# Differential attention: the scores of both maps matmul by matmul in turn on the two halves of TensorE's rows

## The chip, the cores and the metric

One NeuronCore of a Trainium2 chip runs the program. The metric is the device time of one execution in microseconds; the time shown for a kernel is the median of its runs.

## The reference

A decoder trunk of two layers over 528 tokens (16 learned ones ahead of 512) with 1024 channels, all float32. Each layer is half a SwiGLU feed-forward, a mixing sub-layer, and another half feed-forward. The mixing sub-layer projects the normalised input once and gives the parts to two groups of four heads: retention (rq, rk, rv, rg) and differential attention (dq, dk, dv). The change touches the differential group, cut here to what matters:

```
for nb in range(n_blocks):                       # query blocks of 128 (the first has 16 tokens)
    n_keys = (nb + 1) * CHUNK
    qb = q[:, :, :, nb * CHUNK:(nb + 1) * CHUNK] # two maps of 64 channels per head
    s = jnp.einsum('bhmid,bhmjd->bhmij', qb, k[:, :, :, :n_keys]) * scale
    allowed = (kj[None, :] <= qi[:, None]) & (kj[None, :] >= pad)
    p = jax.nn.softmax(jnp.where(allowed, s, -1e30), axis=-1)
    a = p[:, :, 0] - lam * p[:, :, 1]
    outs.append(jnp.einsum('bhij,bhje->bhie', a, v[:, :, :n_keys]))
```

Each head has two score maps; each contracts 64 channels. A softmax is taken of each, and the second, times lambda, is subtracted from the first. The result multiplies the values, and each head's output is normalised.

## The kernel before

Every float32 operand of a matmul is split into a high and a low part, and a product is three matmuls: high x high, low x high, high x low. Activations lie with channels on partitions and tokens along the free dimension, so q and k of one head are tiles of 128 partitions: map 0 on partitions 0 to 63, map 1 on 64 to 127. A score matmul takes 64 of them as its contraction rows.

A layer's mixing stage is `mix_heads`. `proj(name, hd)` computes one projection of one head: 8 channel blocks x 3 products x 2 spans of 264 tokens, 48 matmuls at line 274 (in layer 1 the query-side ones have one span of 512). `evac_rope` takes dq and dk out of PSUM on ScalarE and VectorE, rotates them with four small DMAs and a GpSimd step, and splits them. `evac_v` writes dv to one buffer `vT`, and `v_tokens` (line 691) transposes it.

`diff_scores(hd, mp)` computes one map of one head. Five query blocks (four in layer 1, where the first 16 tokens aren't needed) have 16, 144, 272, 400 and 528 keys. The 528-key block goes to the pair of PSUM banks A in two spans of 264, the others to the pair B: six and twelve matmuls (nine in layer 1), all at line 699. VectorE adds the mask and takes the row maximum while it copies the scores out (line 733), map 0 to the tile `p0`, map 1 to `a_pad`, one buffer each. ScalarE takes the exponentials with the row sums (called at line 741; the profile shows the helper's line 260). `diff_scale` scales map 0 by the reciprocal of its sums on ScalarE (line 759) and then, for map 1, forms map 0 minus lambda times map 1 on VectorE into `a_pad` (line 761). `diff_turn` transposes `a_pad` in two halves (line 785) and splits the result (lines 788 and 792). `pv` multiplies by the values (line 818), and ScalarE copies the output out (lines 826 and 827). `head_norm` sums its squares over channels by matmuls (line 392) and scales.

PSUM has two tags of two buffers, each buffer a pair of banks: `pm` for projections and `pa` for all that is named here.

The loop over heads issues, for head hd with nxt = hd + 1: dq and dk of nxt, v_tokens(hd), the two halves of diff_turn(hd), the front (scores and scaling) of map 0 of nxt, pv(hd), the front of map 1 of nxt, head_norm(hd), dv of nxt. The order in the source is a priority: a scheduler simulates the engines when the program is built, and moves an instruction ahead of one that it holds not to be ready, so that projections fill gaps. On the chip each engine then runs its list in that fixed order.

Of the kernel before, what the change touches and what calls it, by code (L numbers as in the profile page):

```python
# [8 lines left out]
F32 = mybir.dt.float32  # L9
F32R = mybir.dt.float32r  # L10
AF = mybir.ActivationFunctionType
ALU = mybir.AluOpType
# [3 lines left out]
T = 528  # L16
# [41 lines left out]
DIFF_N = [16 + 128 * i for i in range(5)]  # L58
DIFF_OFF = [sum(DIFF_N[:i]) for i in range(5)]
PAD_OFF = [64 * i * (i + 1) for i in range(5)]  # L60
# [137 lines left out]
def trunk(ctx, tc, hT, gains, wgu, wd, win, wout, gnw, sublnw, lam, ret_cs, diff_cs, dtab, mask, out):  # L198
    nc = tc.nc
# [48 lines left out]
    nosync = mybir.DependencyInfo(mybir.DependencyClass.NoSync, mybir.DependencyReason.DATA)  # L248
# [10 lines left out]
    def act_fn(**kw):  # L259
        i = nc.scalar.activation(**kw)  # L260
        tc.add_manual_dep(i.ins, tables["load"].ins.name, nosync, reason="table order")
        tables["users"].append(i)
# [4 lines left out]
    def pair(tag="pa"):  # L267
        return psum.tile([128, 1024], F32, tag=tag, name=tag)
# [19 lines left out]
    def project(mode, srcs, tag="pm"):  # L288

        ps = pair(tag)  # L290
        for k in range(0, len(srcs), 8):
            accumulate(ps, mode, srcs[k:k + 8], W.take(), k, len(srcs))
        return view(ps, mode)
# [22 lines left out]
    blocks, t4 = {}, {}  # L316
# [90 lines left out]
    def norm_end(mode):  # L407
        rsqrt_into(cols(r, mode), col_sum(sums.pop(0), mode), D, mode)
# [205 lines left out]
    def mix_heads(l, mode_next, yh, yl):  # L614
        with tc.tile_pool(name=f"mix{l}", bufs=1, reuse_waits="tile") as pool:
# [6 lines left out]
            a_pad = pool.tile([128, 1920], F32, name="a_pad")  # L622
            msk = acc
# [10 lines left out]
            def scale_cs(kind):  # L634
                for t in cs[kind]:
                    nc.vector.tensor_tensor(out=t, in0=t, in1=r, op=ALU.mult)
# [5 lines left out]
            qk, vv, probs, gate, yn = {}, {}, {}, {}, {}  # L642
# [54 lines left out]
            def scores(out_, pairs, lc, rc, after=None):  # L697
                for n, (a, b) in enumerate(pairs):
                    mm = nc.tensor.matmul(
                        out=out_, lhsT=a[:, lc:lc + 128], rhs=b[:, rc[0]:rc[1]],  # L700
                        start=n == 0, stop=n == len(pairs) - 1,
                    )
                    if n == 0 and after is not None:
                        tc.add_manual_dep(mm.ins, after.ins.name, nosync, reason="one group at a time in a bank")
                return mm

            blocks_i = (4, 3, 2, 1) if q0 else (4, 3, 0, 2, 1)
            i0 = 1 if q0 else 0

            def diff_scores(hd, mp):  # L710
                lp = slice(64 * mp, 64 * mp + 64)
                (qh, ql), (kh, kl) = ([t[lp] for t in qk[n, hd]] for n in ("dq", "dk"))
                A, B = pair(), pair()
                last = {}
                where = {4: A[:, 248:776], 3: B[:, 0:400], 0: B[:, 400:416], 2: B[:, 512:784], 1: B[:, 784:928]}
                for ib in blocks_i:
                    lc = 16 + 128 * (ib - 1) if ib else 0
                    o = where[ib]
                    parts = ((0, 264), (264, 528)) if ib == 4 else ((0, DIFF_N[ib]),)
                    for c0, c1 in parts:  # L720
                        last[ib] = scores(
                            o[:, c0:c1], ((qh, kh), (ql, kh), (qh, kl)), lc, (c0, c1), last.get({0: 3, 1: 2}.get(ib))
                        )
                if mp == 0:
                    s = pool.tile([128, 1360], F32, tag="p0", name="p0")
                    reg = [s[:, DIFF_OFF[i]:DIFF_OFF[i] + DIFF_N[i]] for i in range(5)]
                else:
                    reg = [a_pad[:, PAD_OFF[i] + 112:PAD_OFF[i] + 112 + DIFF_N[i]] for i in range(5)]
                mx = pool.tile([128, 5], F32, tag="mx", name="mx", bufs=3)
                ls = pool.tile([128, 5], F32, tag="ls", name="ls", bufs=4)  # L730
                for ib in blocks_i:
                    n = DIFF_N[ib]
                    nc.vector.tensor_tensor_reduce(
                        out=reg[ib], in0=where[ib],
                        in1=msk[:, T - n:T] if ib else msk[:, 400:416], scale=1.0, scalar=-3e38,
                        op0=ALU.add, op1=ALU.max, accum_out=mx[:, ib:ib + 1],
                    )
                mx, ls = mx[:, i0:], ls[:, i0:]
                nc.vector.tensor_scalar(out=mx, in0=mx, scalar1=-0.125, scalar2=None, op0=ALU.mult)
                for ib in blocks_i:  # L740
                    act_fn(
                        out=reg[ib], in_=reg[ib], func=AF.Exp, scale=0.125, bias=mx[:, ib - i0:ib - i0 + 1],
                        accum_out=ls[:, ib - i0:ib - i0 + 1],
                    )
                probs[hd, mp] = (reg, ls)

            def diff_scale(hd, mp):
                reg, ls = probs[hd, mp]
                nc.vector.reciprocal(out=ls, in_=ls)
                if mp == 1:  # L750
                    nc.vector.tensor_scalar(
                        out=ls, in0=ls, scalar1=nlam[:, l:l + 1], scalar2=None, op0=ALU.mult
                    )
                    reg0 = probs.pop((hd, 0))[0]
                    probs.pop((hd, 1))
                for ib in sorted(blocks_i):
                    lc = ls[:, ib - i0:ib - i0 + 1]
                    if mp == 0:
                        nc.scalar.activation(out=reg[ib], in_=reg[ib], func=AF.Copy, scale=lc)
                    else:  # L760
                        nc.vector.scalar_tensor_tensor(
                            out=reg[ib], in0=reg[ib], scalar=lc, in1=reg0[ib],
                            op0=ALU.mult, op1=ALU.add,
                        )
# [118 lines left out]
            def evac_gate(hd, ps):  # L883
                gate[hd] = cols(a_pad[:, hd * T:(hd + 1) * T] if hd < 3 else swap, qm)
                nc.vector.tensor_tensor(out=gate[hd], in0=ps, in1=cols(r, qm), op=ALU.mult)
# [11 lines left out]
            def load_decay(hd):  # L897
                dtabs[hd] = row(const, "acc1" + "hl"[hd % 2])
                nc.sync.dma_start(out=dtabs[hd], in_=dtab[hd])
# [3 lines left out]
            def proj(name, hd):  # L903
                ps = project(qm if name in ("dq", "rq", "rg") else FULL, xs, "pa" if len(first) == 2 else "pm")
                first.append(name)
                if len(first) == 1:
                    norm_end(FULL)
                    scale_cs("d")
                if name in ("dq", "dk", "rq", "rk"):
                    evac_rope(name, hd, ps)  # L910
                elif name == "rg":
                    evac_gate(hd, ps)
                else:
                    evac_v(name, hd, ps)

            def diff_front(hd, mp):
                diff_scores(hd, mp)
                diff_scale(hd, mp)

            for name in ("dq", "dk", "dv"):  # L920
                proj(name, 0)
            load_cs("r", ret_cs)
            scale_cs("r")
            load_decay(0)
            diff_front(0, 0)
            diff_front(0, 1)
            for hd in range(HEADS):
                nxt = hd + 1
                if nxt < HEADS:
                    proj("dq", nxt)  # L930
                    proj("dk", nxt)
                else:
                    proj("rq", 0)
                    proj("rk", 0)
                v_tokens("dv", hd)
                diff_turn(hd, 0)
                diff_turn(hd, 1)
                if nxt < HEADS:
                    diff_front(nxt, 0)
                    pv("dv", hd)  # L940
                    diff_front(nxt, 1)
                    head_norm("dv", hd)
                    proj("dv", nxt)
                else:
                    vT["rv"] = pool.tile([128, 640], F32, tag="vT", name="vTr")
                    nc.gpsimd.memset(vT["rv"][:, T:640], 0.0)
                    proj("rv", 0)
                    ret_scores(0)
                    pv("dv", hd)
                    v_tokens("rv", 0)  # L950
                    ret_split(0)
                    head_norm("dv", hd)
            for hd in range(HEADS):
                nxt = hd + 1
# [55 lines left out]
    for i, k in enumerate(PAIRED):  # L1010
# [9 lines left out]
        out=ident, in_=ident, pattern=[[-1, 128]], compare_op=ALU.is_equal, fill=0.0, base=0,  # L1020
# [11 lines left out]
    for l in range(DEPTH):  # L1032
        last = l == DEPTH - 1
# [104 lines left out]
```

## Time and profile before

| | |
|---|---|
| median of 3 runs | 2092.46 us (2090.86 to 2094.35) |
| profiled execution, its time | 2090.78 us |
| its span, first to last instruction | 2089.1 us |
| TensorE matmuls, busy | 2012.6 us (96%) |
| VectorE, busy | 1557.1 us (75%) |
| ScalarE, busy | 964.7 us (46%) |
| GpSimd, busy | 393.5 us (19%) |
| mean granted clock of TensorE | 0.991 of 2.4 GHz |

Busy time is the union of an engine's instructions; weight loads overlap matmuls and are counted apart. Matmuls are pipelined, so the time that one takes from the stream is read from start to start and not from its duration.

### The profile page before, as it was taken

The numbers are of one execution on the slowest core, as the hardware profiler recorded it, in microseconds if no ns is written. First come the engines' busy times: TensorE is split into PE (matmuls) and PEld (weight loads), VectorE is DVE, ScalarE is ACT, GpSimd is POOL, SyncE is SP. The second block draws the span as 40 slices with busy tenths as digits, with TensorE's granted clock in tenths as the row PEclk, the third lists the DMA queues.
The fourth block names the chain that finished last, engine by engine and source line by source line (L and its number), as shares of the span: only waits on it lengthen the run. The fifth ranks groups of instructions, "written<-read, shape, count | busy, mean of one in ns | idle before, by whom it ended". The sixth has DMA issues, their size and how long they took to land. (4 is left out here: it accounts for less than half of the span.)

```text
span 2089.1 us, 36950 instructions
## 1 busy us (share of the span) xinstructions
PE 2012.6 (96%) x15262; PEld 1938.1 (93%) x15262; DVE 1557.1 (75%) x2278; ACT 964.7 (46%) x1502; POOL 393.5 (19%) x274
## 2 busy tenths in 40 slices
PE   7999999999999999999989999999999999999996
PEld 7999999999999999999989999998888878898995
DVE  8758766777777876967698686766777788696765
ACT  7424434455436543534555253344553455353443
POOL 0101000444343200100110010014433241010102
PEclk9999999999999999999999999999999999999998
DMA  5232323311212232232223133133211123333231
GB/s 178 97 102 78 115 82 92 125 58 63 71 53 91 92 122 73 92 121 73 89 97 124 64 105 126 61 94 112 68 59 62 61 82 100 101 101 122 80 104 49
DMA packets 57513, 190.10 MB, mean 91 GB/s; under 512 B 7040, under 2 KB 9088, under 8 KB 57344
## 3 DMA queue, kind: packets, MB, share of 16 engines
q1 hardware_dynamic: 56320, 186.66, 27.2%
q8 instruction: 120, 1.97, 0.4%
q10 hardware_dynamic: 1024, 1.08, 0.3%
q14 instruction: 49, 0.40, 0.1%
HBM read 184.53 MB, written 2.10 MB: 89 GB/s over the span
## 5 line engine op out<-in xcount | busy, mean ns | idle before, releaser
L124 POOL TENSOR_TENSOR ws<-ws,wraw 128x512 f32<-128x512 f32 x78 | 122.1, 1566 | 1114.1 <-DVE ws L123 816.7
L99 ACT ACTIVATE whi<-wraw 128x1024 fp32r<-128x1024 f32 (+1 forms) x183 | 187.4, 1032 | 270.1 <-PE pm L274 148.2
L491 PE MATMUL pm<-XH,xhi 128*128 128x264 f32 (+1 forms) x828 | 238.6, 288 | 12.3 <-DVE gu L542 6.9
L491 PE MATMUL pm<-XH,xlo 128*128 128x264 f32 (+1 forms) x828 | 235.8, 285 | 0.0
L491 PE MATMUL pm<-XL,xhi 128*128 128x264 f32 (+1 forms) x828 | 235.8, 285 | 0.0
L491 PE MATMUL pm<-XH,whi 128*128 128x264 f32 (+1 forms) x732 | 210.3, 287 | 7.2 <-DVE gu L469 6.2
L100 DVE TENSOR_TENSOR wlo<-wraw,whi 128x1024 fp32r<-128x1024 f32 (+1 forms) x151 | 188.2, 1248 | 29.3 <-ACT whi L99 28.5
L491 PE MATMUL pm<-XH,wlo 128*128 128x264 f32 (+1 forms) x732 | 207.8, 284 | 0.0
L491 PE MATMUL pm<-XL,whi 128*128 128x264 f32 (+1 forms) x732 | 207.5, 283 | 0.0
L274 PE MATMUL pm<-XH,whi 128*128 128x264 f32 (+1 forms) x768 | 182.2, 305 | 8.8 <-DVE ra L668 7.8
L274 PE MATMUL pm<-XH,wlo 128*128 128x264 f32 (+1 forms) x768 | 179.8, 303 | 0.0
L274 PE MATMUL pm<-XL,whi 128*128 128x264 f32 (+1 forms) x768 | 179.8, 303 | 0.0
L491 PEld LDWEIGHTS pm<-XH,xhi 128*128 128x128 f32 x828 | 156.7, 189 | 17.5 <-DVE gu L469 6.1
L491 PEld LDWEIGHTS pm<-XH,xlo 128*128 128x128 f32 x828 | 157.1, 190 | 0.3
L491 PEld LDWEIGHTS pm<-XL,xhi 128*128 128x128 f32 x828 | 157.1, 190 | 0.0
L491 PEld LDWEIGHTS pm<-XH,whi 128*128 128x128 f32 x732 | 138.1, 189 | 10.1 <-DVE gu L469 8.3
L274 PEld LDWEIGHTS pm<-XH,whi 128*128 128x128 f32 x768 | 125.0, 191 | 16.4 <-ACT whi L99 3.7
L99 ACT ACTIVATE xhi<-ws 128x1024 fp32r<-128x1024 f32 x82 | 86.8, 1059 | 112.2 <-PE pm L491 38.8
L491 PEld LDWEIGHTS pm<-XH,wlo 128*128 128x128 f32 x732 | 138.4, 189 | 0.2
L491 PEld LDWEIGHTS pm<-XL,whi 128*128 128x128 f32 x732 | 138.3, 189 | 0.0
L274 PEld LDWEIGHTS pm<-XL,whi 128*128 128x128 f32 x768 | 124.7, 191 | 4.7
L274 PEld LDWEIGHTS pm<-XH,wlo 128*128 128x128 f32 x768 | 124.6, 191 | 4.5
(266 smaller groups left out, 6060.7 us busy)
## 6 DMA issues: line engine op xcount, KB each, us to landing
wraw<-in_wgu SPq DMA_DIRECT2D x176, 512.0 KB
wraw<-in_wd SPq DMA_DIRECT2D x66, 512.0 KB
wraw<-in_win SPq DMA_DIRECT2D x56, 512.0 KB
wraw<-in_wd SPq DMA_DIRECT2D x32, 384.0 KB
wraw<-in_wout SPq DMA_DIRECT2D x16, 512.0 KB
slabs<-in_hT SPq DMA_DIRECT2D x8, 264.0 KB
out_y<-slabs SPq DMA_DIRECT2D x8, 256.0 KB
acc1h<-in_dtab SPq DMA_DIRECT2D x4, 264.0 KB
```

The costliest lines, as they stand in the source:

```text
L99: self.nc.scalar.activation(out=hi, in_=t, func=AF.Copy)
L100: (eng or self.nc.vector).tensor_tensor(out=lo, in0=t, in1=hi.bitcast(F32), op=ALU.subtract)
L124: nc.gpsimd.tensor_tensor(out=s4, in0=s2, in1=a12, op=ALU.add)
L274: nc.tensor.matmul(out=ps[:, o:o + c1 - c0], lhsT=a, rhs=b[:, c0:c1], start=start and n == 0, stop=stop and n == 2,)
L491: nc.tensor.matmul(out=out_, lhsT=p[:, s], rhs=q, start=k == 0 and n == 0 and what in ("P1", "P2", "P7"), stop=k == 3 and n == 2, skip_gro ...
```

## The change

One call of `diff_scores(hd, part)` now serves both maps. Part 0 computes the 528-key block of both, part 1 the other blocks of both; each part takes two pairs of banks, one for each map. Within a part the matmuls go map 0, map 1, map 0, map 1, and each depends in the schedule on the one before it, without a semaphore, so that the scheduler keeps them in that order. The copies out with mask and maximum follow each part. The exponentials and `diff_scale` of both maps follow part 1. Around it, dv of the next head moves ahead of part 1, and for head 0 dq of head 1 moves between the two parts.

```
-            def diff_scores(hd, mp):
-                lp = slice(64 * mp, 64 * mp + 64)
-                A, B = pair(), pair()
...
+            def diff_scores(hd, part):
...
+                P = [pair(), pair()]
+                if part == 0:
+                    where = [{4: t[:, 248:776]} for t in P]
+                else:
+                    where = [{3: t[:, 0:400], 0: t[:, 400:416], 2: t[:, 512:784], 1: t[:, 784:928]} for t in P]
...
+                for ib in blocks:
...
+                    for c0, c1 in spans:
+                        for n, (x, y) in enumerate(((0, 0), (1, 0), (0, 1))):
+                            for mp in range(2):
+                                q, k = ops[mp]
+                                mm = nc.tensor.matmul(
+                                    out=where[mp][ib][:, c0:c1], lhsT=q[x][:, lc:lc + 128], rhs=k[y][:, c0:c1],
+                                    start=n == 0, stop=n == 2,
+                                )
...
+                                if "turn" in last:
+                                    tc.add_manual_dep(mm.ins, last["turn"].ins.name, nosync, reason="maps in turn")
+                                last[mp, ib] = last["turn"] = mm
+                for mp in range(2):
...
+                    for ib in blocks:
+                        n = DIFF_N[ib]
+                        nc.vector.tensor_tensor_reduce(
...
+                if part == 0:
+                    return
+                for mp in range(2):
...
+                    for ib in blocks_i:
+                        act_fn(
+                            out=reg[ib], in_=reg[ib], func=AF.Exp, scale=0.125, bias=mx[:, ib - i0:ib - i0 + 1],
...
+                    diff_scale(hd, mp)
...
-            diff_front(0, 0)
-            diff_front(0, 1)
+            diff_scores(0, 0)
+            proj("dq", 1)
+            diff_scores(0, 1)
             for hd in range(HEADS):
                 nxt = hd + 1
                 if nxt < HEADS:
-                    proj("dq", nxt)
+                    if hd:
+                        proj("dq", nxt)
                     proj("dk", nxt)
...
                 if nxt < HEADS:
-                    diff_front(nxt, 0)
+                    diff_scores(nxt, 0)
                     pv("dv", hd)
-                    diff_front(nxt, 1)
+                    proj("dv", nxt)
+                    diff_scores(nxt, 1)
                     head_norm("dv", hd)
-                    proj("dv", nxt)
```

## Rows read from the trace of the kernel before

**Rows 1.** The page's first part: each engine's busy time in us, share, instructions.

```profile
PE 2012.6 (96%) x15262; PEld 1938.1 (93%) x15262; DVE 1557.1 (75%) x2278; ACT 964.7 (46%) x1502; POOL 393.5 (19%) x274
```

**Rows 2.** Busy times in the differential heads' stretches of layers 0 and 1.

```profile
395.00:545.00 150.00, 145.96 (x1146) 140.92 (x1145) 112.61 (x219) 77.66 (x174) 62.19 (x43) 1.00 0.22 71
1428.00:1582.00 154.00, 144.81 (x973) 131.21 (x972) 119.03 (x209) 74.11 (x155) 62.42 (x45) 0.99 0.22 69
```

**Rows 3.** TensorE's waits in these stretches: us in total, times, longest.

```profile
PE pm L274 <- DVE ra L668: 3.1, 2, 1.7
...
PE pm L274 <- DVE ra L668: 4.7, 3, 1.8
PE pa L785 <- DVE a_pad L761: 1.7, 2, 1.3
```

**Rows 4.** TensorE's matmuls around one map's scores: start, us, line, shapes, count.

```profile
444.24 0.41 PE L274 MATMUL pm<-XL,whi 128*128 128x264 f32 x2
444.58 0.39 PE L699 MATMUL pa<-kh,qh 64*128 64x264 f32 x1
444.81 0.28 PE L699 MATMUL pa<-kh,ql 64*128 64x264 f32 x1
...
445.29 0.28 PE L699 MATMUL pa<-kl,qh 64*128 64x264 f32 x1
445.50 0.51 PE L274 MATMUL pm<-XH,whi 128*128 128x264 f32 x2
445.84 0.29 PE L274 MATMUL pm<-XH,wlo 128*128 128x264 f32 x1
446.06 0.45 PE L699 MATMUL pa<-kh,qh 64*128 64x400 f32 x1
446.35 0.34 PE L699 MATMUL pa<-kh,ql 64*128 64x400 f32 x1
446.53 0.34 PE L699 MATMUL pa<-kl,qh 64*128 64x400 f32 x1
...
447.17 0.29 PE L699 MATMUL pa<-kh,ql 64*128 64x272 f32 x1
447.30 0.28 PE L699 MATMUL pa<-kl,qh 64*128 64x272 f32 x1
...
447.80 0.39 PE L274 MATMUL pm<-XH,wlo 128*128 128x264 f32 x1
```

**Rows 5.** Weight loads of the 16-column block and the next, same map.

```profile
446.71 0.18 PEld L699 LDWEIGHTS pa<-kh,ql 64*128 64x128 f32 x1
446.82 0.19 PEld L699 LDWEIGHTS pa<-kl,qh 64*128 64x128 f32 x1
446.93 0.19 PEld L699 LDWEIGHTS pa<-kh,qh 64*128 64x128 f32 x1
```

**Rows 6.** ScalarE in one head: exponentials, pv's output copied, map 0 scaled.

```profile
452.18 0.74 ACT L260 ACTIVATE p<-p,mx 128x528 f32<-128x528 f32 x1 [6.42 <-DVE mx L739]
...
454.73 0.59 ACT L826 ACTIVATE osb<-pa 128x528 f32<-128x528 f32 x1
...
456.24 2.16 ACT L759 ACTIVATE p<-p,ls 128x16 f32<-128x16 f32 x5
```

**Rows 7.** TensorE in this head: map 1's last score, the next turn's first transpose.

```profile
458.52 0.27 PE L699 MATMUL pa<-kl,qh 64*128 64x144 f32 x1
...
467.11 0.27 PE L785 MATMUL pa<-ident,a_pad 128*128 128x128 f32 x1
```

**Rows 8.** VectorE in this head: map 1's second part copied out, first and last.

```profile
458.83 0.57 DVE L733 CUSTOM_DVE_ANT_0 a_pad<-pa,acc 128x400 f32<-128x400 f32 x1 [3.78 <-PE pa L699]
...
460.01 0.08 DVE L733 DVE_READ_ACCUMULATOR2_ANT mx<- 128x1 f32 x1
```

More of the change, by code (lines that the diff above doesn't have):

```diff
@@ L708, in mix_heads @@
             i0 = 1 if q0 else 0
-            def diff_scores(hd, mp):
-                lp = slice(64 * mp, 64 * mp + 64)
-                (qh, ql), (kh, kl) = ([t[lp] for t in qk[n, hd]] for n in ("dq", "dk"))
-                A, B = pair(), pair()
+            def diff_scores(hd, part):
+                ops = [
+                    [[t[64 * mp:64 * mp + 64] for t in qk[n, hd]] for n in ("dq", "dk")] for mp in range(2)
+                ]
+                P = [pair(), pair()]
[3 more added lines that the diff above has]
+                    where = [{3: t[:, 0:400], 0: t[:, 400:416], 2: t[:, 512:784], 1: t[:, 784:928]} for t in P]
+                blocks = [ib for ib in blocks_i if ib in where[0]]
@@ L714, in diff_scores @@
                 last = {}
-                where = {4: A[:, 248:776], 3: B[:, 0:400], 0: B[:, 400:416], 2: B[:, 512:784], 1: B[:, 784:928]}
-                for ib in blocks_i:
+                for ib in blocks:
                     lc = 16 + 128 * (ib - 1) if ib else 0
[L718 to L722, printed above, removed]
-                        )
@@ L724, in diff_scores @@
[L724 to L745, printed above, removed]
+                    spans = ((0, 264), (264, 528)) if ib == 4 else ((0, DIFF_N[ib]),)
@@ new lines, in diff_scores @@
+                    for c0, c1 in spans:
[6 more added lines that the diff above has]
+                                )
+                                after = last.get((mp, {0: 3, 1: 2}.get(ib)))
+                                if n == 0 and after is not None:
+                                    tc.add_manual_dep(
+                                        mm.ins, after.ins.name, nosync, reason="one group at a time in a bank"
+                                    )
+                                if "turn" in last:
+                                    tc.add_manual_dep(mm.ins, last["turn"].ins.name, nosync, reason="maps in turn")
+                                last[mp, ib] = last["turn"] = mm
@@ new lines, in diff_scores @@
+                for mp in range(2):
+                    if part == 0:
+                        if mp == 0:
+                            s = pool.tile([128, 1360], F32, tag="p0", name="p0")
+                            reg = [s[:, DIFF_OFF[i]:DIFF_OFF[i] + DIFF_N[i]] for i in range(5)]
+                        else:
+                            reg = [a_pad[:, PAD_OFF[i] + 112:PAD_OFF[i] + 112 + DIFF_N[i]] for i in range(5)]
+                        mx = pool.tile([128, 5], F32, tag="mx", name="mx", bufs=3)
+                        ls = pool.tile([128, 5], F32, tag="ls", name="ls", bufs=4)
+                        probs[hd, mp] = (reg, ls, mx)
+                    reg, ls, mx = probs[hd, mp]
+                    for ib in blocks:
+                        n = DIFF_N[ib]
+                        nc.vector.tensor_tensor_reduce(
+                            out=reg[ib], in0=where[mp][ib],
+                            in1=msk[:, T - n:T] if ib else msk[:, 400:416], scale=1.0, scalar=-3e38,
+                            op0=ALU.add, op1=ALU.max, accum_out=mx[:, ib:ib + 1],
+                        )
@@ new lines, in diff_scores @@
+                if part == 0:
+                    return
+                for mp in range(2):
+                    reg, ls, mx = probs[hd, mp]
+                    mx, ls = mx[:, i0:], ls[:, i0:]
+                    nc.vector.tensor_scalar(out=mx, in0=mx, scalar1=-0.125, scalar2=None, op0=ALU.mult)
+                    for ib in blocks_i:
+                        act_fn(
+                            out=reg[ib], in_=reg[ib], func=AF.Exp, scale=0.125, bias=mx[:, ib - i0:ib - i0 + 1],
+                            accum_out=ls[:, ib - i0:ib - i0 + 1],
+                        )
+                    probs[hd, mp] = (reg, ls)
+                    diff_scale(hd, mp)
@@ L914, in proj @@
                     evac_v(name, hd, ps)
-            def diff_front(hd, mp):
-                diff_scores(hd, mp)
-                diff_scale(hd, mp)
             for name in ("dq", "dk", "dv"):
```

## The prediction

> **What bounds the kernel now.** I read the page's first part, then two stretches of the trace that hold the differential heads of the two layers, then the order on TensorE inside one head. TensorE's matmuls cover 96% of the span and the next engine, VectorE, 75% [rows 1]. In the two stretches TensorE is busy 145.96 of 150 us and 144.81 of 154 us, and VectorE 112.61 and 119.03 [rows 2]. So TensorE sets the end there too, and time taken from it shortens the kernel as long as nothing else comes late. The list of waits says how near that is: in the first layer's heads the longest total is 3.1 us, for the evacuation of a projection, in the second 4.7 us for the same and 1.7 us for transposes that wait for the softmax's last step [rows 3]. The waits are small but there, and those of the second layer say that the chain from one head's scores to its transposes is already nearly as long as the work that hides it.
>
> **What the scores cost.** One map's scores run as two islands among projection matmuls [rows 4]. Projection matmuls start 0.12 us apart (two to a row, rows 0.24 apart). In the first island six matmuls of 264 columns start 0.12 us apart (444.81 to 445.29 is four steps). In the second the 400-column ones start 0.18 apart, the 272-column ones 0.13. The short ones, 16 and 144 columns, are paced by the weight loads, which follow each other 0.11 us apart although a 16-column stream is far shorter [rows 5].
>
> Around an island there is more. From the last two projection matmuls to the first score 0.34 us pass where two take 0.24; from the first score to the second 0.23 where 0.12 would do; from the last score to the next projection 0.21; and the first two projections after it take 0.34 [rows 4]. That is 0.10 + 0.11 + 0.09 + 0.10 = 0.40 us for going from 128 rows to 64 and back, once an island.
>
> The first island lasts 444.58 to 445.50 and the second 446.06 to 447.80 [rows 4]: 0.92 and 1.74 us, each with 0.20 of that 0.40 inside. Streaming is thus 0.72 + 1.54 = 2.26 us a map. The second layer has no 16-column block, three steps of 0.11 fewer: 1.93. Eight maps each: 18.1 + 15.4 = 33.5 us, and 32 islands x 0.40 = 12.8 us. The scores hold 46 us, 2.2% of the span; nothing the change does to them directly can be worth more than about half.
>
> **The change, part by part.** *Fewer islands.* Both maps' 528-key block becomes one run of twelve matmuls, the rest one of 24 (18 in layer 1). Their order is chained, and once the banks are free every operand is there, so I count them as whole: two islands a head in place of four, 16 fewer, 16 x 0.40 = 6.4 us saved. If projections are put between them this is gone.
>
> *Map by map in turn.* No row shows two neighbours on different halves of the rows, so I bound it. At best two neighbours take the time of one: half of 33.5, 16.7 us. At worst each of the alternations, 11 + 23 a head in layer 0 and 11 + 17 in layer 1, 248 in all, drains the array as entering or leaving an island does (0.20): 50 us lost. Between them lies what [rows 5] point to: loads for 64 rows still come 0.11 us apart, one behind the other. If that stays so across the halves, a pair can't be faster than 2 x 0.11 = 0.22 us, however well the streams overlap. Then 264 columns gain 0.02 a pair (0.24 to 0.22), six pairs: 0.12; 400 columns 0.36 to 0.22, three pairs: 0.42; 272 columns 0.26 to 0.22, three pairs: 0.12; 16 and 144 columns nothing. That is about 0.6 us a head, 5 us over eight. I take this: of the three it is the one nearest to a row, since the load spacing is seen, and neither two loads at once nor a drain inside 64-row work is.
>
> The Trainium skill, page "TensorEngine Tiling (Array Packing)", section Tiling Modes, says that a change of tiling mode drains TensorE, a change of tile within a mode does not, and that different tiles can load weights and multiply in parallel. The trace agrees on the first (0.40 us an island) and has nothing on the others. By that rule the alternation would save the 16.7 us of the best case, not 5.
>
> *What moves.* The same vector and scalar instructions run, in another order. Before, map 0's exponentials ran before pv's output was copied: from 452.18 to 454.73, 2.55 us, with the copy of pv's output right behind them [rows 6]. Now no exponential runs before the second part's scores, so that copy, and the bank it frees, come up to 2.55 us sooner. But all of map 0's later work now lands behind the last score. Today the last score starts at 458.52 and the first transpose of the next turn at 467.11, 8.6 us later [rows 7]. Added to that: map 0's reductions of the short blocks, 1.26 us as map 1's from 458.83 to the last read's end at 460.09 [rows 8]; its exponentials, 2.55; its five scaling copies, 2.16 [rows 6]. That is 6.0 us, 14.6 in all. Over it lie dq and dk of the head after next, 48 matmuls x 0.12 = 5.8 us each, and five transposes of v and four matmuls of column sums, 1 us at the same step: 12.7. The next head's dv, another 5.8, can be pulled ahead by the planner as the island gaps show that it pulls projections ahead: 18.5. So it is covered, with little to spare. For head 0, whose dq(1) now stands between its two parts, only dk(1) and dv(1) cover it: 11.6 + 1 against 14.6. Two heads x about 1 to 2 us: I take 2 us lost in all. The planner's rearrangement of weight splits and rotary steps on VectorE and ScalarE I cost at nothing, since they have about 25% and 50% idle time in these stretches [rows 2]; if they fall into the chain they add to it.
>
> dv(nxt) moves ahead of the second part, where it covers the copy of pv's output. Its own evacuation needs v's buffer, free since the transposes of v of this head. No DMA is added; the weights' order is that of the projections, which differs in nothing but dq(1) and dv, so SP's queue stays as it is. Banks: two pairs per part, as two pairs per map before.
>
> Sum: 6.4 + 5 - 2 = 9.4 us saved. The profiled execution took 2090.8 us, so 2081.4; the median of the runs is 1.7 us above that execution, so 2083.
>
> **Rivals.** *Full overlap*, chance 0.22. Two halves load and stream together: 6.4 + 16.7 = 23.1 us off TensorE, 2.9 a head. Then the 18.5 us of cover shrinks against a chain that doesn't, and I take 2 + 4 us lost to it (0.5 a head): 17 us, 2075. For it: the streams touch different rows and different bank pairs. Against it: the load spacing.
>
> *The chain eats the gain*, 0.18. If 1.4 us a head (11.4 / 8) goes into waiting for the transposes, nothing is left: 2092. For it: the second layer has 1.7 us of such waits already [rows 3].
>
> *Slower through the same chain*, 0.15: the transposes of a turn wait for a softmax that ends 6.0 us later, and the planner, which has simulated times only, doesn't pull dv ahead. Without dv the cover is 12.7 against 14.6, and 1 us more of splits in between makes 3 us a head: 24 - 11.4 = 13 slower, 2105. It decides from 1.4 us of new waiting a head upwards. Against it: pv's copy comes 2.55 sooner, and the first layer has almost no such waits today.
>
> *Each alternation drains*, 0.05: 50 - 6.4 = 43 us slower, 2136. Nothing in the trace speaks for it but the price of entering and leaving.
>
> **The numbers.** My forecast has 0.40, with its own range of 2078 to 2088 (the alternation worth 2 to 8 us, the head-0 loss 1 to 4). The range of 2072 to 2100 leaves out the drain (0.05), the worst two thirds of the slower chain (0.10) and the best quarter of the full overlap (0.05). 0.2% of this kernel is 4.2 us, about what a measurement can tell from no change. Faster: 0.40 + 0.22 = 0.62; same: 0.17 out of the rival that ends even; slower: 0.15 + 0.05 + 0.01 = 0.21.
>
> **What would show it.** Right: in each head two 64-row runs of 12 and 24 (18) matmuls; starts inside them 0.11 us apart on the mean, loads 0.11 apart, about 4 us a head in place of 4.5; waits of the transposes for the last softmax step up by no more than 2 us. Full overlap shows as starts in pairs, about 0.06 us apart on the mean. A drain shows as 0.2 us between starts. The chain rival shows in the waits of TensorE for the softmax's last step and for the projections' evacuation growing by 10 us or more. I am wrong in the first step if projections split the runs.

## The result: 2126.19 us, 34.5 us slower

| | before | after |
|---|---|---|
| median of 4 runs | 2091.66 us (2089.95 to 2094.35) | 2126.19 us (2122.53 to 2127.34) |
| span of the profiled execution | 2089.1 us | 2123.9 us |
| mean granted clock of TensorE | 0.991 | 0.983 |

The ratio is 1.0162, 95% interval 1.0150 to 1.0175. The forecast was 2083.0 in a range of 2072 to 2100: wrong in sign, and beyond the range.

The page's first part and the windows of the two heads' stretches, after, answer to [rows 1] and [rows 2]:

```profile
PE 2011.3 (95%) x15262; PEld 1931.6 (91%) x15262; DVE 1556.5 (73%) x2278; ACT 962.8 (45%) x1502; POOL 386.1 (18%) x274
```

```profile
395.00:545.00 150.00, 134.45 (x1077) 128.49 (x1075) 101.01 (x185) 63.95 (x139) 54.51 (x38) 0.95 0.22 68
1428.00:1582.00 154.00, 137.34 (x945) 123.47 (x943) 105.58 (x173) 67.30 (x132) 58.54 (x45) 0.96 0.25 78
```

No engine has more to do. In the same 150 and 154 us every engine gets less done, and the granted clock falls from 1.00 and 0.99 to 0.95 and 0.96. That is the picture of waiting, not of work. TensorE's waits in these stretches, after, against [rows 3] (first layer, then second):

```profile
PE pm L274 <- DVE ra L668: 6.9, 5, 2.0
PE pa L844 <- DVE mx L754: 5.0, 1, 5.0
...
PE pa L729 <- DVE XL L818: 6.1, 2, 5.7
PE pm L274 <- DVE ra L668: 4.9, 5, 1.6
PE pa L811 <- DVE a_pad L787: 1.9, 1, 1.9
```

Transposes that wait for the softmax's last step (L811), the wait that the prediction watched, hold 1.9 us. The growth stands elsewhere: pv (L844) and scores (L729) wait for a pair of banks that VectorE hasn't emptied, 5.0 and 5.7 us at a time. The kernel before had a small wait of this kind in the same stretch of layer 1, which [rows 3] don't show:

```profile
PE pa L699 <- DVE XL L792: 1.7, 1, 1.7
```

Over the whole run scores wait 8.0 us for this split, against 3.2, and projections 17.2 us for their banks (L668), against 7.8.

**The overlap is there in full.** TensorE's matmuls in the same head as [rows 4], then its weight loads (as [rows 5]):

```profile
446.82 0.39 PE L729 MATMUL pa<-kh,qh 64*128 64x264 f32 x1
...
448.43 0.38 PE L729 MATMUL pa<-kh,qh 64*128 64x264 f32 x1
448.43 0.50 PE L729 MATMUL pa<-kh,ql 64*128 64x264 f32 x2
448.66 0.40 PE L729 MATMUL pa<-kl,qh 64*128 64x264 f32 x2
448.78 0.40 PE L729 MATMUL pa<-kh,qh 64*128 64x264 f32 x2
...
455.49 0.44 PE L729 MATMUL pa<-kh,qh 64*128 64x400 f32 x1
...
459.37 0.44 PE L729 MATMUL pa<-kh,qh 64*128 64x400 f32 x1 [0.20 <-ACT sqh L853]
459.37 0.62 PE L729 MATMUL pa<-kh,ql 64*128 64x400 f32 x2
459.66 0.52 PE L729 MATMUL pa<-kl,qh 64*128 64x400 f32 x2
```

```profile
448.54 0.30 PEld L729 LDWEIGHTS pa<-kl,qh 64*128 64x128 f32 x2
448.66 0.30 PEld L729 LDWEIGHTS pa<-kh,qh 64*128 64x128 f32 x2
```

A row with x2 is one matmul of each map; what starts together is a product of map 1 and the next product of map 0. A pair follows a pair after 0.12 us at 264 columns and 0.18 at 400, as one matmul followed another before: two for the price of one, the loads too. But a lone first score (446.82, 455.49) stands 1.6 and 3.9 us ahead of its part, with projections between. The scheduler put them there. At 455.49 the chip bears it out: the rest of the part waits until ScalarE has copied pv's output out of the other pair. At 446.82 it doesn't: the last split that empties the second pair ended at 445.44 on VectorE. So most heads still have four islands (30 in all, where the kernel before has 32).

**Where the time went.** I split the mixing stage of both layers (from 150 matmuls ahead of the layer's first score to the feed-forward's first matmul) from start to start of TensorE's matmuls. A step's due time is its columns at 2.4 per ns plus 12 ns, which fits [rows 4] (0.122 us at 264, 0.179 at 400), and at least 112 ns, as the loads of [rows 5] are spaced. What a gap holds beyond that is a stall if it is over 0.3 us, and half clock where a step is near twice its due; all else is streaming. Each row is one execution, and executions of one kernel lie 4 to 12 us apart (e15: 2090.22 to 2101.95). Sums of both layers, us:

| kernel | streaming | stalls | half clock | both stages |
|---|---|---|---|---|
| before | 529.8 | 20.5 | 12.7 | 563.0 |
| after | 515.4 | 59.5 | 19.8 | 594.7 |
| e6_defer_forced | 527.4 | 30.5 | 12.6 | 570.5 |
| e13_one_map_then_other | 526.6 | 31.9 | 11.6 | 570.1 |
| e4_softmax_per_part | 515.0 | 45.4 | 12.8 | 573.2 |
| e11_all_one_pair | 510.0 | 41.6 | 15.0 | 566.6 |
| e15_one_pair_no_turns | 515.5 | 34.4 | 9.9 | 559.8 |
| e9_first_block_only | 523.9 | 28.2 | 10.6 | 562.7 |
| e14_first_block_no_turns | 524.8 | 15.1 | 7.1 | 547.0 |
| e10_before_early | 527.3 | 15.0 | 8.4 | 550.7 |
| e16_more_streaming | 539.2 | 19.5 | 10.3 | 569.0 |

The change takes 14.4 us of streaming off TensorE and pays 39.0 of stalls and 7.1 of half clock. The border between streaming and half clock is rough: some 5 to 6 us of each entry under half clock are steps near twice their due while the clock was granted in full, an island's second step (0.23 us in [rows 4]) among them. Taken by the granted clock of the trace, half clock is 7.9 us before and 17.2 after, and streaming falls by 16.6.

**One stall.** TensorE, then VectorE in head 2 of layer 0, then two windows there (us; busy of PE, PEld, DVE, ACT, POOL; granted clock; DMA):

```profile
485.60 0.37 PE L729 MATMUL pa<-kl,qh 64*128 64x264 f32 x2
490.99 0.56 PE L844 MATMUL pa<-XH 128*128 128x272 f32 x1 [5.03 <-DVE mx L754]
...
494.58 0.41 PE L844 MATMUL pa<-XH,XL 128*128 128x256 f32 x1
494.79 0.41 PE L844 MATMUL pa<-XL,XH 128*128 128x256 f32 x1
```

```profile
482.63 2.22 DVE L818 TENSOR_TENSOR XL<-pa,XH 128x400 fp32r<-128x400 f32 x4
484.78 2.12 DVE L873 SCALAR_TENSOR_TENSOR osb<-osb,sub,ro 128x528 f32<-128x528 f32 x1
486.82 0.69 DVE L671 TENSOR_TENSOR ra<-ra,rb 128x528 f32<-128x528 f32 x1
487.44 1.21 DVE L150 TENSOR_REDUCE wmu<-wraw 128x8 f32<-128x1024 f32 x1
488.68 1.42 DVE L659 TENSOR_TENSOR rb<-pm,acc0l 64x528 f32<-64x528 f32 x2
490.13 0.71 DVE L754 CUSTOM_DVE_ANT_0 p<-pa,acc 128x528 f32<-128x528 f32 x1
```

```profile
486.00:491.00 5.00, 0.01 (x1) 0.04 (x1) 4.92 (x8) 1.26 (x2) 2.89 (x3) 0.59 0.34 105
491.00:498.00 7.00, 7.00 (x30) 6.54 (x31) 2.97 (x6) 1.11 (x2) 0.89 (x1) 0.50 0.00 0
```

The last scores of the 528-key block start at 485.60 and hold both pairs of `pa`. Neither is free until VectorE copies it out at 490.13, because its fixed list has an output's last step, a rotation and a weight's sums ahead. pv, which needs a pair, stands 5.03 us; VectorE is busy 4.92 of the 5.00 us from 486 to 491. Behind the wait the granted clock is 0.50, 1.2 of 2.4 GHz: pv's 256-column steps are 0.21 us apart in place of 0.12. The 5.7 us wait of layer 1 is of the same kind: scores at 1537.77 wait for the last split (L818), which stands on VectorE behind an output's last steps, a weight split and a weight's sums.

### The profile page after: what moved, and what is told of

It is laid out like the page before. It is cut to its first block, busy times and chain, and to the rows that moved or that the text cites. A ratio compares the mean times of both kernels' runs of the same rounds, so it can differ in the third digit from the quotient of the medians.

```text
span 2123.9 us, 36958 instructions
## 1 busy us (share of the span) xinstructions
PE 2011.3 (95%) x15262; PEld 1931.6 (91%) x15262; DVE 1556.5 (73%) x2278; ACT 962.8 (45%) x1502; POOL 386.1 (18%) x274
## 5 line engine op out<-in xcount | busy, mean ns | idle before, releaser
L491 PE MATMUL pm<-XH,xhi 128*128 128x264 f32 (+1 forms) x828 | 238.3, 288 | 14.9 <-DVE gu L542 6.9
L274 PE MATMUL pm<-XH,whi 128*128 128x264 f32 (+1 forms) x768 | 185.8, 311 | 21.7 <-DVE ra L668 17.2
L274 PEld LDWEIGHTS pm<-XH,whi 128*128 128x128 f32 x768 | 127.2, 195 | 33.1 <-issue 10.5
```

The lines of the kernel that those rows point to most:

```text
L274: nc.tensor.matmul(out=ps[:, o:o + c1 - c0], lhsT=a, rhs=b[:, c0:c1], start=start and n == 0, stop=stop and n == 2,)
L491: nc.tensor.matmul(out=out_, lhsT=p[:, s], rhs=q, start=k == 0 and n == 0 and what in ("P1", "P2", "P7"), stop=k == 3 and n == 2, skip_gro ...
```

## The experiments

Each was timed beside the kernel before on the same chip (2093 to 2094.5 us there); the ratio to it has its 95% interval. The scheduler plans every kernel anew, so an edit can also shift instructions of other engines. None leaves work out. The runs that split the softmax or the copies out add small instructions on VectorE, and the last adds matmuls.

**Which part of the change costs?** *e1_no_pin*: the change without the chain that pins the order of the score matmuls. *e2_map_by_map*: pinned, but the three products of one map, then those of the other.

```
e1: - if "turn" in last: tc.add_manual_dep(mm.ins, last["turn"].ins.name, ...)
e2: - for n, (x, y) in enumerate(...):        + for mp in range(2):
    -     for mp in range(2):                 +     for n, (x, y) in enumerate(...):
```

> The changed kernel without the chain that pins the score matmuls' order. Theory A (the softmax of both maps stands behind the last score, so the loop from one head's transposes to the next got longer than TensorE's work): the chain is as long as before, 2118 to 2132 us. Theory B (the pinned order and the two pairs of banks that a part needs at once split the runs and keep the scheduler from filling): most of the loss comes back, 2090 to 2105 us. Theory C (the moved projections leave the gaps without cover): no change, 2120 to 2132.

> The changed kernel with the two loops swapped: inside a block the three products of map 0, then those of map 1, so that only every third pair of neighbours lies on different halves of the rows; all else as in the change. If TensorE's time still sets the end, the overlap lost (about 2/3 of 17 us) is added: 2135 to 2145. Theory A: TensorE waits for the chain anyway, most of it disappears in the waits: 2122 to 2133.

e1: 2100.81 us, 1.0034 (1.0021 to 1.0047). Left free, the scheduler puts map 0 ahead of map 1 in heads 1 to 3. e2: 2108.66, 1.0073 (1.0052 to 1.0095). e1 lies in the range of theory B, e2 below both of its ranges. Both are far faster than the change, but neither is a clean test of the overlap (see e12).

*e3_softmax_late* is the kernel before with both maps' exponentials and scaling written behind map 1's copies; *e5_moves_only* is the kernel before with the change's moves of dq(1) and dv.

```
e3: (diff_front)  + if mp == 1:
                  +     for m in range(2): diff_exp(hd, m); diff_scale(hd, m)
e5: + proj("dq", 1)   ...   + if hd: proj("dq", nxt)   ...   + proj("dv", nxt)  ahead of map 1's front
```

> The kernel before, with one thing of the change alone: the exponentials and scaling of map 0 are issued behind map 1's scores instead of ahead of them. Scores map by map, projections where they were. Theory A: the loss comes from this, 2110 to 2130 us. Theories B and C: nothing of what they blame is in it, 2088 to 2098 us.

> The kernel before with the moved projections alone: dq of head 1 between the two maps of head 0, dv of the next head ahead of map 1's scores. Theory C: 2105 us or more. Theories A and B: 2088 to 2098 us.

e3: 2092.43, 0.9997 (0.9986 to 1.0008). e5: 2094.16, 1.0004 (0.9995 to 1.0014). The scheduler gave e3 the engines' lists of the kernel before, so it tests nothing. In the trace of e5, too, every engine's operations come in the order of the kernel before, but for one place on ScalarE, as far as names and shapes tell them apart. So what the moves cost inside the change is not shown by e5; e13 below has them, and is 10.1 us slower than before in all. To force e3's order, *e6_defer_forced* pins map 0's negated maxima behind map 1's last copy:

```
+ tc.add_manual_dep(neg.ins, copied[hd].ins.name, nosync, reason="softmax behind both maps")
```

> The kernel before, scores map by map, with one added order: map 0's negated maxima, and so its exponentials, come behind the last copy-out of map 1 on VectorE. The earlier run that only changed the source order left the engines' lists as they were; this one forces it. Theory A: 2105 to 2125 us. Theory B: 2090 to 2100 us.

e6: 2102.18, 1.0042 (1.0027 to 1.0058): the late softmax by itself costs 8.4 us by the medians, where I had taken 2; that lies between the two ranges. *e4_softmax_per_part* undoes part of it in the change: the 528-key block's exponentials and scaling stand right behind its part.

```
- if part == 0:
-     return
+ c = slice(4, 5) if part == 0 else slice(i0, 4)      # this part's columns of mx and ls
```

> The changed kernel, but the 528-key block's softmax (negated maxima, exponentials, reciprocals, scaling, difference) is issued right behind part 0 for both maps, so that only the shorter blocks' softmax stands behind part 1. Theory A (the softmax behind both maps lengthens the loop): 40% of it leaves the chain, at least a third of the 34 us comes back, 2095 to 2114 us. Theory B (pinned parts that need both pairs of banks at once): little changes, 2118 to 2130 us.

e4: 2107.28, 1.0066 (1.0042 to 1.0091), 19 us faster than the change, as theory A had it: stalls fall by 14.1, half clock by 7.0, streaming stays. How much of that is a gain of any kernel, e10 below tells.

**Banks.** *e7_one_pair* cuts the second part in two, {400, 16 keys} and {272, 144 keys}, each with both maps in one pair of banks. *e8_one_pair_early* is e7 with e4. *e11_all_one_pair* is e8 with each 264-key span of the 528-key block in one pair for both maps.

```
e7:  + elif part == 1:
     +     t = pair()
     +     where = [{3: t[:, o:o + 400], 0: t[:, o + 400:o + 416]} for o in (0, 512)]
e11: + where = [{4: [t[:, o:o + 264] for t in P]} for o in (0, 512)]
```

> The changed kernel, but part 1 is cut in two, and each half holds both maps in one pair of banks (map 0 in its first bank, map 1 in its second): blocks of 400 and 16 keys, then blocks of 272 and 144. Turns and chained order within a part stay, softmax late as in the change. Theory B: the runs no longer need two free pairs at once, at least half of the loss comes back, 2095 to 2110 us. Theory A: the softmax is as late as before, 2118 to 2130 us.

> Both of the two above: each later part in one pair of banks, and the 528-key block's softmax right behind part 0. If both causes are real and the overlap is worth some 12 us of TensorE's time, it beats the kernel before: 2078 to 2090 us. If only one is, it stands where that one's own run stands.

> The run with one pair per later part and early softmax, with part 0 changed too: each 264-key span of the 528-key block holds both maps in one pair of banks, at the price of two more copies-out and two small maxima a head on VectorE (about 0.7 us). If the lone first score ahead of each part 0 and its wait for a second pair is what still costs, 2088 to 2096; if VectorE's queue is what costs, 2100 to 2108.

e7: 2111.32, 1.0086 (1.0071 to 1.0101), 15 us faster than the change. e8: 2098.90, 1.0025 (1.0016 to 1.0034). e11: 2095.82, 1.0010 (1.0001 to 1.0018). e7 lies between its two ranges, e8 above its own, e11 in the first of its two. Taking one pair in place of two for the later parts is worth 15 us with the late softmax (change to e7) and 8 with the early one (e4 to e8), and the same for the first block 3 more (e8 to e11). But with 20 us of streaming gone (510.0 against 529.8) e11 only draws level with the kernel before, and it has the early softmax, which gains by itself (e10): beside e10, timed on the same chip, it is 10.5 us slower with 17.3 us less streaming.

**Is it the turns or what came with them?** Turns are the two maps' matmuls in alternation. *e12_one_pair_map_by_map* swaps e11's two inner loops as e2 does, meant to take the overlap away at the same banks.

> The run in which every pair of banks holds both maps, with the two loops swapped: three products of map 0, then three of map 1, so that most of the overlap is gone and nothing else is. If TensorE's time sets the end in the heads, the lost overlap is added: 2104 to 2110 us against 2096. If the chain of softmax, transposes and bank releases sets it, it stays within 3 us of 2096.

e12: 2095.97, 1.0009 (0.9999 to 1.0018), but its premise fell. TensorE's matmuls there, whose list, by the source and its chain, has three of map 0, then three of map 1:

```profile
452.14 0.46 PE L733 MATMUL pa<-kh,qh 64*128 64x400 f32 x2
452.43 0.35 PE L733 MATMUL pa<-kh,ql 64*128 64x400 f32 x2
452.61 0.35 PE L733 MATMUL pa<-kl,qh 64*128 64x400 f32 x2
```

They start in pairs, 10 ns apart: the other half's matmuls start ahead of two older ones. *e13_one_map_then_other* goes further, in the change itself: all of map 0 in a part, then all of map 1.

```
- for ib in blocks:                            + for mp, ib in [(mp, ib) for mp in range(2) for ib in blocks]:
-             for mp in range(2):              +             for _ in (0,):
```

> The changed kernel with all of map 0's matmuls of a part ahead of all of map 1's, still chained: same parts, banks, softmax and projections, no turns and no overlap (some 14 us more of streaming). If the turns cost because map 0's copies-out wait for map 1, this is well below the changed kernel although TensorE works longer: 2098 to 2112 us. If the order inside a part doesn't matter, 2126 or, with TensorE as the bound, 2138.

e13: 2103.19, 1.0038 (1.0025 to 1.0051), in the first range, 23 us faster than the change with 11.2 us more streaming. Its heads run islands of 6, 6, 12 and 12 (9 and 9 in layer 1; head 0 apart), nearly all without pairs; stalls are 27.6 us fewer and half clock 8.2.

*e9_first_block_only* keeps turns for the 528-key block only; the other blocks go map by map as before, the softmax is e4's. *e14_first_block_no_turns* is e9 with e13's edit: map 0's six, then map 1's six. *e10_before_early* has no turns: the kernel before with the 528-key block's softmax split off as in e4.

```
e9:  + maps = range(2) if part == 0 else (part - 1,)
     + P = {mp: pair() for mp in maps}
e10: + for c, blocks in ((slice(4, 5), [4]), (slice(i0, 4), blocks_i[1:])):   # exponentials and scaling
```

> Only the 528-key block of both maps runs in turn; the rest of map 0 and the rest of map 1 run each by itself in one pair, map 0's ahead of pv and map 1's behind it as in the kernel before, and projections stand where they stood. Each block group's softmax is issued right behind its copy-out. If the loss came from what the turns make wait (map 0's softmax and two pairs at once) and not from the turns themselves, this keeps a third of the overlap (6 us) and loses little: 2084 to 2096 us, beside 2094 of before. If the turns themselves cost, above 2100.

> The run in which only the 528-key block of both maps took turns (2097), now with map 0's six matmuls ahead of map 1's six: no turns left anywhere, the rest the same. If the turn itself is what keeps that run above the 2085 of the kernel before with early softmax, 2084 to 2090. If it is that both maps' blocks go first and need both pairs, 2095 to 2103.

> The kernel before, scores map by map, with only the softmax of the 528-key block issued apart from the other blocks' (its own negated maximum, exponential, reciprocal and scaling). A control for the run with the softmax per part: if that run's gain was the chain put right and not a gain of any kernel, this one is within 4 us of before (2090 to 2098). If early softmax gains by itself, 2082 to 2090.

e9: 2097.09, 1.0014 (1.0005 to 1.0023). e14: 2081.17, 0.9942 (0.9928 to 0.9955). e10: 2085.33, 0.9960 (0.9945 to 0.9974). e9 lies between its two ranges and e14 below both of its own. e10 lies in the second: early softmax gains 8 us by itself, so that much of e4's 19 is no repair of the change. Taking the turns out of one block makes it 16 us faster. TensorE in the same head, e9:

```profile
444.24 0.39 PE L732 MATMUL pa<-kh,qh 64*128 64x264 f32 x1
...
445.72 0.38 PE L732 MATMUL pa<-kh,qh 64*128 64x264 f32 x1
...
446.32 0.40 PE L732 MATMUL pa<-kl,qh 64*128 64x264 f32 x2
...
458.73 0.44 PE L732 MATMUL pa<-kh,qh 64*128 64x400 f32 x1 [1.45 <-DVE mx L757]
```

and e14:

```profile
444.72 0.39 PE L732 MATMUL pa<-kh,qh 64*128 64x264 f32 x1
...
445.44 0.28 PE L732 MATMUL pa<-kl,qh 64*128 64x264 f32 x1
...
446.21 0.38 PE L732 MATMUL pa<-kh,qh 64*128 64x264 f32 x1
...
455.88 0.45 PE L732 MATMUL pa<-kh,qh 64*128 64x400 f32 x1
```

Their copies out of the 528-key block on VectorE, and the first of map 0's other blocks, e9 and e14:

```profile
447.99 0.70 DVE L757 CUSTOM_DVE_ANT_0 p<-pa,acc 128x528 f32<-128x528 f32 x1
...
448.62 0.70 DVE L757 CUSTOM_DVE_ANT_0 a_pad<-pa,acc 128x528 f32<-128x528 f32 x1
...
455.73 0.56 DVE L757 CUSTOM_DVE_ANT_0 p<-pa,acc 128x400 f32<-128x400 f32 x1
```

```profile
446.35 0.70 DVE L757 CUSTOM_DVE_ANT_0 p<-pa,acc 128x528 f32<-128x528 f32 x1
...
447.60 0.70 DVE L757 CUSTOM_DVE_ANT_0 a_pad<-pa,acc 128x528 f32<-128x528 f32 x1
...
452.85 0.56 DVE L757 CUSTOM_DVE_ANT_0 p<-pa,acc 128x400 f32<-128x400 f32 x1
```

e9's first score stands alone at 444.24, with eight projection matmuls between it and the rest of its block. The list has them there, not a wait: the last split of the transposes before, which empties the second pair, ended on VectorE at 444.21. Both maps are done only at 446.7, and the copies start at 447.99. In e14 map 0 runs whole, its copy starts 1.64 us sooner, its pair is emptied while map 1 is computed, and map 1's other blocks start at 455.88 with no wait in place of 458.73 behind 1.45 us. That last step is not the turns' own: map 0's other blocks start at 450.0 in both kernels, and VectorE copies them out from 455.73 in e9 and from 452.85 in e14, because its list differs.

**What is a microsecond of streaming worth?** *e15_one_pair_no_turns* is e11 with all of map 0 in a span (first part) or part ahead of map 1. *e16_more_streaming* is the kernel before with the first product of every group issued twice.

```
e15: + for mp, ib, spans in todo:             # map 0's blocks, then map 1's
e16: + again = nc.tensor.matmul(out=o[:, c0:c1], lhsT=qh[:, lc:lc + 128], rhs=kh[:, c0:c1], start=True, stop=True)
```

> This is e11_all_one_pair (every span or block of both maps in one pair of banks, the softmax of the 528-key block right behind the first part; 2095.8 us) with the turns taken out: in a span of the first part and in the whole second part map 0's matmuls all stand ahead of map 1's. Nothing is left out. Map by map swaps of three matmuls (e12) left the overlap in place, since the array starts the other half's matmuls ahead of their place; with runs of 9 to 12 on one half most of the overlap must go. Expected in the trace: starts of one map 0.12 us apart at 264 columns and 0.18 at 400, no pairs except where the two runs meet, and TensorE's own work in the heads up by 10 to 13 us over e11's. If the streaming of the scores sets the end, the time goes up by as much, to 2104 to 2110. If the chain of copies-out, softmax and transposes sets it, the stalls go down by about what the streaming goes up, and the time stays within 3 us of 2096 or falls below it, as it did from e9 to e14.

> The kernel before, with the first of each group of three score products (high x high) issued twice, each time from the start of its group, so the output is unchanged and only TensorE's streaming is repeated. By before's steps (0.12 us at 264 columns, 0.18 at 400, 0.13 at 272, 0.11 at 144 and 16) this adds 0.77 us a map in layer 0 and 0.66 in layer 1, eight maps each: 11.4 us. If TensorE's streaming sets the end in the heads, as the prediction's first step has it, the time goes up by all of it, to 2104 or 2105. If the chain from the scores to the transposes sets it there, part of the 11.4 us is taken from waits, but the last scores and so the chain also come later: within 4 us of 2093. Then what the turns save in streaming could never have been worth more than that.

e15: 2096.40, 1.0014 (1.0001 to 1.0026). In its trace half the pairs are still there, since spans of three are too short and the array starts ahead here too; 5.5 us of streaming came back in place of 10 to 13. The median is e11's: as far as it goes, the chain's side. The table has 7.2 us less of stalls and 5.1 less of half clock for e15, but these can't be set against the streaming: its profiled execution (2090.22 us) was its fastest, e11's (2096.95) one of its slowest.

e16: 2104.54, 1.0053 (1.0035 to 1.0071): 11.1 us (7.3 to 14.9) by this ratio and 10.1 by the medians, for 11.4 us of added work. Its profiled execution shows a smaller price: the span grows by 10.1, the two mixing stages by 6.0 (streaming 9.4 more, stalls and half clock 3.4 less), and the other 4.1 lie where nothing was edited. So added streaming is paid at a price between half and the whole. In the kernel before TensorE does set most of the end: this refutes what the runs ahead of it had led me to think, that the chain does already.

## Why the prediction was wrong

**The step that failed** is the condition in the first: "time taken from it shortens the kernel as long as nothing else comes late". That TensorE sets the end in the kernel before holds for the most part, by e16. That nothing comes late does not: I allowed 2 us for it, and stalls grew by 39.0 and half clock by 7.1. The line that let it through is "Banks: two pairs per part, as two pairs per map before": in the kernel before the pairs of a map are filled one behind the other, and each can be emptied when its own six or twelve matmuls are through; here a part needs both at once and fills both to its end. That I put at nothing.

**The scores' cost and the islands.** The first gain, 6.4 us for 16 islands fewer, did not come: each part was cut into a lone score and the rest, as the prediction's own proviso had it, because the second map's banks come free later, in the scheduler's plan and in part on the chip. I had written "once the banks are free every operand is there" and not asked when *both* pairs are.

**Map by map in turn.** I took 5 us, since loads of one half came 0.11 us apart. They do, but the two halves load side by side, and a pair costs one matmul. Streaming fell by 14.4 us, near the 16.7 of the bound that I called full overlap. That rival's mechanism was right; its time was not. The Trainium skill, page "TensorEngine Tiling (Array Packing)", section Tiling Modes, has the rule that different tiles load and multiply in parallel. The trace agrees: loads and matmuls of the two halves start together, 0.12 us a pair at 264 columns.

**What moves.** The chain from last score to transposes was foretold at 14.6 us. The same head after, TensorE's ends of it, then VectorE's and ScalarE's steps between, as [rows 6 to 8]:

```profile
460.91 0.27 PE L729 MATMUL pa<-kl,qh 64*128 64x144 f32 x1
...
475.16 1.04 PE L811 MATMUL pa<-ident,a_pad 128*128 128x128 f32 x8
```

```profile
463.16 0.56 DVE L754 CUSTOM_DVE_ANT_0 p<-pa,acc 128x400 f32<-128x400 f32 x1
...
465.51 0.28 DVE L764 TENSOR_SCALAR mx<-mx 128x5 f32<-128x5 f32 x2
...
473.30 2.14 DVE L787 SCALAR_TENSOR_TENSOR a_pad<-a_pad,ls,p 128x16 f32<-128x16 f32 x5
```

```profile
457.67 0.65 ACT L679 ACTIVATE kh<-ra 128x528 fp32r<-128x528 f32 x1 [4.96 <-DVE ra L671]
458.22 0.59 ACT L852 ACTIVATE osb<-pa 128x528 f32<-128x528 f32 x1
...
465.71 0.74 ACT L260 ACTIVATE p<-p,mx 128x528 f32<-128x528 f32 x1 [4.90 <-DVE mx L764]
```

It is 14.25 us here. But I looked for its loss where it ends, at the transposes (1.9 us), and it appears where the next work wants banks or VectorE's time. ScalarE idles 4.90 us ahead of the first exponential, then both maps' softmax comes in one lump. pv's output is copied at 458.22, 11.4 us behind the head's first score, where it was 10.15 [rows 4, 6]: the 2.55 us that I saw freed were not used. pv's last matmul starts at 455.29, but ScalarE's list has a split of the next keys ahead of the copy, and that split waits 4.96 us for VectorE's rotary step. And "the planner's rearrangement ... I cost at nothing" because VectorE has 25% idle: what counted was the order in its list. In the 5.03 us stall it was busy nearly throughout, with other work of its list.

**The two prices.** From the kernel before, the late softmax alone costs 8.4 us (e6). The change without its turns costs 10.1 (e13), and the turns on top bring it to 34.5: 24.4 more, although they take 11.2 us of streaming away. So the turns are the larger part, and the late softmax most of the rest. The price of the turns hardly depends on when the softmax comes: with the early one the change (e4) stands 22 us above the kernel without turns (e10), though these two differ in more than the turns. And e4's 19 us are about what the softmax's place is worth without turns (e6 to e10, 17).

**The rivals.** "Slower through the same chain" had the right sign and named its point, 1.4 us a head; but it placed the wait at the transposes and gave 2105. Of the two waits that it named as its sign, 10 us or more together, the transposes' grew by 0.2 us and the evacuations' (L668) by 9.4. No case had a part that holds both pairs at once.

**How long the bank pairs are held.** From the first score in a pair of banks to the end of the last copy out of it, the four pairs of a head (mean of heads 1 to 3 of both layers) are held 11.3 us in all before, 22.8 after, 12.9 in e13, 18.1 in e9 and 13.2 in e14. For map 0 this splits at its last score:

| map 0, us | 528 keys: first to last score | last score to copy | other blocks: first to last score | last score to copy |
|---|---|---|---|---|
| before | 0.72 | 1.57 | 1.37 | 0.83 |
| after | 3.09 | 1.80 | 5.43 | 1.63 |
| e13 | 0.71 | 2.24 | 1.38 | 0.79 |

So in the change a pair of banks is held longer because map 0's scores start early and end late, and hardly because VectorE comes later behind the last one.

**Left open.** Why the rest of a part starts so long after its first score: the scheduler's list and real waits for the second pair both do it, and no kernel was run with the lists of the other engines held. From e9 to e14, too, VectorE's list changed with the turns. And e16 and e11 stand side by side unreconciled in size: 11.4 us more cost about all, while 17.3 us less than e10 came with 10.5 us of loss.

## What to carry to other kernels

Before crediting streaming time saved, ask when the work's outputs can start, and when they come free: two row tiles in turn need two accumulators at once and finish both late, where one after the other hands the first on while the second runs. With only two bank pairs for a whole chain, handing on early was worth more (16 us on one block, e14 against e9, VectorE's changed list included) than two matmuls for one. The better versions here have no turns and split the softmax: the largest block's exponentials right behind its own copy (e10, 0.9960 of the kernel before; e14, which also computes both maps' largest blocks first, 0.9942).

## What the hardware showed that I had not expected

Matmuls on the two halves of the rows load weights and stream side by side: starts of a pair lie up to 10 ns apart, pairs 0.12 us apart at 264 columns and 0.18 at 400, as single ones do. TensorE does not keep its list's order across the halves, though I had written that each engine runs its list in a fixed order: with three matmuls of one half ahead of three of the other they started as pairs (e12); with six or more, separated by projections, they did not (e13). And a wait of 5 us cost more than itself: behind it the clock was granted at 0.50 (1.2 GHz) through at least 491 to 498 us.
